# Low-rank and gate matrices of a diffusion block padded with zero rows to 128

## The chip, the cores and the metric

The kernel runs on one core of one Trainium2 chip. Its time is device microseconds of one execution. Three runs of the kernel before gave 2284.68, 2291.41 and 2297.06 us; the median, 2291.41 us, is its time. In the profile, PE is TensorE's matmul, PEld its weight load, DVE VectorE, ACT ScalarE, POOL GpSimd and SP the engine that issues most transfers.

## The reference

One layer of a hybrid diffusion backbone over 256 latent tokens and 256 context tokens, 2048 channels wide: a modulated norm, one input projection, two token mixers side by side (a bidirectional RWKV-7 scan with 16 heads of 64, and a bidirectional chunked gated DeltaNet with 8 heads of 128), a gated merge, an output projection and a SwiGLU feed-forward block. The change touches the RWKV features and readout:

```
lora_w = einsum('btdr,drc->btdc', tanh(wd.reshape(b, t, 2, 96)), w2)      # 2 directions, rank 96
decay  = exp(-exp(-softplus(-(w0 + lora_w)) - 0.5))
iclr   = sigmoid(a0 + einsum('btdr,drc->btdc', ad.reshape(b, t, 2, 96), a2))
gate   = sigmoid(gd) @ g2                                                 # rank 64
...
return (yn + bonus) * gate
```

`wd` and `ad` are 2 x 96 columns each of the input projection, `gd` is 64 columns, and each of `w2`, `a2` and `g2` maps a rank to 1024 channels.

## The kernel before, in words

Activations lie with channels on the 128 partitions and tokens along the free dimension: 512 tokens (latent, then context), or the 256 latent ones.

The first stage (to about 132 us) makes the modulation vectors and the modulated activations, and accumulates in six PSUM tiles, `low`, the first projections: four groups of 96 low-rank columns among them, with 64 gate columns and 32 DeltaNet columns in the rows that are left over. The last two stages (from about 1312 us) merge the branches, project and run the feed-forward block. They consist of projections in three products each: weights and activations are split into a high and a low part in fp32r, high x high, high x low and low x high.

The stage between is where the change lies. Its order on PE, DVE, ACT and POOL is not that of the code: generators yield operations, and a planner, `Weave`, picks at each step the operation that could start first by its own books, with a rank to break ties. Its books hold a cost for each operation (`Lane.__getattr__`), a time at which each engine is free, and events that generators wait for. A matmul's cost is a fixed share plus so much per column, with a factor 1.22 for 96 rows (L137); an operation on POOL costs 0.06 + 0.0024 us per element of a partition. Each engine then runs its instructions in the planned order and waits on semaphores where the data is not there. SP is left to the framework's own scheduler.

The generators of that stage:

- `lowrank` (L718) makes the activations of the four low-rank groups. `shift` mixes each token with its neighbours, with one operation on ACT and six on DVE, and writes 96 rows of `lin`, a view of a tile with the tag KB. Then it works in four bursts of eight products of 96 rows: for each pair `p` of RWKV heads four products `w[:96]` by `lin`, out to one of two PSUM banks with the tag s (`psb`). Each is emptied by `lowrank_out` (L710): a sigmoid on ACT into `lo`, then a write to DRAM issued from ACT. One load of `lora` serves a burst. Before the second burst it makes `sgd`, the 64 rows of the gate's activations.
- `prepare`, `grams`, `inverse`, `values` and `scan` run the eight pairs. The first `prepare` waits for its pair's low-rank rows, the second one for all of them. At the end of `scan` (L983 to L987) stands the gate product: a load of 64 rows of `g2`, one product with `sgd`, 256 columns wide, and a copy by ACT.
- `features`, `tokens`, `decays`, `head_grams`, `head_inverse` and `head_scan` run the eight DeltaNet heads, after the pairs. `ada_rest` runs beside them on DVE.
- `products` (rank 900, last of all) does the remaining input projections. `cast` splits each weight piece into `whi` on ACT and `wlo` on DVE. A projection is 48 matmuls, 512 or 256 columns wide. They are the work that fills PE while the others wait.

All helpers' operations carry line 145, where a planned operation is issued; `dq` loads carry L156. Arrays are laid out on the host: `lora` as 4 x 96 x 8 x 128, `g2` as 64 x 1024.

Of the kernel before, what the change touches and what calls it, by code (L numbers as in the profile page):

```python
# [11 lines left out]
F32 = mybir.dt.float32  # L12
F32R = mybir.dt.float32r
AF = mybir.ActivationFunctionType
# [4 lines left out]
P = 128  # L19
D = 2048  # L20
KT = D // P
T = 256
# [88 lines left out]
class Lane:  # L111
# [5 lines left out]
    def __getattr__(self, name):  # L117

        def op(out, *a, **k):
            if name == "preload_act_table_set":  # L120
                return Op(self, 1.3, lambda: self.engine.preload_act_table_set(out))
            if name == "dma_start":
                return Op(self, 0.6 if self.each > 0.002 else 0.06, lambda: self.engine.dma_start(out, *a))
            n = int(np.prod(out.shape[1:]))
            kind = "full"
            if name == "transpose" and len(a) == 2:
                cost = 0.109
            elif name == "matmul":
                rows, m = a[0].shape[0], out.shape[0]
                if a[0].dtype == F32R:  # L130
                    cost, kind = 0.0035 + 0.000448 * n, "split"
                elif rows <= 64 and m <= 64:
                    cost, kind = 0.026 if rows < 64 else max(0.06, 0.05 + 0.00015 * n), (rows, m)
                elif m <= 64:
                    cost, kind = 0.085 if m == 64 else 0.12, (rows, m)
                else:
                    cost = (0.0054 + 0.00167 * n) * (1.22 if rows == 96 else 1)  # L137
            else:
                psum = a and getattr(a[0], "tensor", None) is not None and "PSum" in type(a[0].tensor).__name__
                cost = (self.psum if psum else self.fixed) + self.each * n  # L140
                if name == "tensor_tensor_scan":
                    cost *= 1.9
                elif name == "scalar_tensor_tensor" and not psum:
                    cost *= 1.2
            return Op(self, cost, lambda: getattr(self.engine, name)(out, *a, **k), kind)  # L145
        return op
# [124 lines left out]
def emit(ctx: ExitStack, tc, A, out, dbg=None):  # L271
    nc = tc.nc
    V, S, G, Q = nc.vector, nc.scalar, nc.gpsimd, nc.sync
# [3 lines left out]
    dq = Loads(Q)  # L277
    e, v, s = Lane(E, 0.0, 0.0, 0.0), Lane(V, 0.07, 0.00104, LAT["own"], 0.13), Lane(S, 0.09, 0.00086, LAT["own"], 0.165)
    g = Lane(G, 0.06, 0.0024, LAT["own"])
# [129 lines left out]
    with tc.tile_pool(name="p0", bufs=1) as p0, \  # L409
# [31 lines left out]
        ps = pst(pa, "pa")  # L441
# [263 lines left out]
    for b in (pib, mmb, psb, psb, mmb, pab):  # L705
        b.free.pop()
    pr[0]["kps"], pr[0]["rps"] = low[4], low[5]
    sgd = rs.tile([64, T], F32, tag="sgd", name="sgd")

    def lowrank_out(p, j, ps, so):  # L710
        yield s.activation(so, ps, AF.Sigmoid, bias=p_("w0" if j < 2 else "a0", 8 * (j % 2) + p))
# [6 lines left out]
    def lowrank():  # L718

        yield s.preload_act_table_set(SIGM)  # L720
        lin = rs.tile([P, 2, 8, 2, 64], F32, tag="KB", name="lin", bufs=2).rearrange("p a b c d -> p (a b c d)")[:96].rearrange("p (j t) -> p j t", j=4)
        raw = rs.tile([P, 4, 64], F32, tag="Y", name="raw").rearrange("p a b -> p (a b)")[:64]
        ab = rs.tile([P, 512], F32, tag="XT", name="ab")[:32]
        for j, b in ((0, pib), (2, psb), (1, mmb), (3, psb)):
            ps = low[j]
            yield from shift(ps, 96, 24 + j, lin[:, j])
            if j < 2:
                yield s.activation(lin[:, j], lin[:, j], AF.Tanh)
                yield s.copy(raw[32 * j:32 * j + 32], ps[96:P, 0:T])
            if j == 2:  # L730
                yield s.copy(ab, ps[96:P])
                Q.dma_start(abd.rearrange("b r t -> r b t"), ab.rearrange("r (b t) -> r b t", b=4))
            weave.release(b)
        out = [rs.tile([P, 8, 2, 64], F32, tag=f"VX{i}", name="lo").rearrange("p a b c -> p (a b c)") for i in range(2)]
        out = [t[:, n:n + 512] for t in out for n in (0, 512)]
        for p in range(NPAIR):
            if p == 2:
                yield from shift(raw, 64, 28, sgd, ctx_part=False)
                yield s.activation(sgd, sgd, AF.Sigmoid)
                yield "prepared", 0, 1  # L740
                yield s.preload_act_table_set(SIGM)
            if p % 2 == 0:
                w = wp.tile([P, 8, P], F32, tag="wraw", name="wraw", bufs=3)
                yield dq(w[:96], A["lora"][p // 2])
            for j in (0, 2, 1, 3):
                ps = yield psb
                yield e.matmul(ps, w[:96, 4 * (p % 2) + j], lin[:, j], start=True, stop=True)
                weave.add(2, lowrank_out(p, j, ps, out[j]))

    def prepare(p):  # L750
# [152 lines left out]
    def scan(p):  # L903
# [76 lines left out]
        weave.ready("scan", p)  # L980

        Yf = Y.rearrange("p c t -> p (c t)")
        g2 = rs.tile([P, P], F32, tag="gate", name="g2")[:64]  # L983
        Q.dma_start(g2, A["g2"][:, P * p:P * p + P])
        ps = yield pab
        yield e.matmul(ps[:, T:], g2, sgd, start=True, stop=True)
# [659 lines left out]
def layouts(x, c, ctx, c_ctx, w_ada, b_ada, norm1_w, w_in, rw_mu, rw_w0, rw_w2, rw_a0, rw_a2,  # L1646
# [67 lines left out]
                                             (3360, 96), (1024, P), (0, P))]  # L1714
    A["w_low"] = np.ascontiguousarray(np.concatenate(lows, 2).reshape(P, 8, 2, 736).transpose(1, 0, 2, 3))
    lw = np.concatenate([np.asarray(rw_w2[0], f), np.asarray(rw_a2[0], f)], 0)
    A["lora"] = np.ascontiguousarray(lw.reshape(4, 96, 4, 2, P).transpose(2, 1, 3, 0, 4)).reshape(4, 96, 8, P)
    A["g2"] = np.asarray(rw_g2[0], f)
    A["pa"] = cols(merge_p_a[0], [P * j for j in range(KT)])
    A["pb"] = cols(merge_p_b[0], [P * j for j in range(KT)])  # L1720
    A["wout"] = cols(w_out[0], [P * j for j in range(KT)])
# [18 lines left out]
```

## Time and profile before

| what | value |
| --- | --- |
| median of three runs | 2291.41 us (2284.68 to 2297.06) |
| profiled execution, its span | 2286.3 us (the page gives no other time of it) |
| mean granted clock of TensorE | 0.985 |
| POOL, busy | 110.3 us |
| DMA queues, share of 16 engines' span | 49.5% SP and ACT, 7.1% POOL, 3.3% a third |

The profile is one execution. A f32 product stands in it as two records with a load each, an fp32r product as one. Matmuls are pipelined, so that a record lasts longer than the distance to the next one: distances between starts tell what a product costs. A row of a group gives the line, engine, operation, out<-in and the shape, where 96*128 means 96 active rows and 128 active columns; then the busy time, the mean in ns, and the idle time of the engine ahead of it with what ended it. A row of the order of time gives start and length in us, and in brackets the idle time ahead of it and its releaser. A row of busy time by stretches gives the stretch, its length, the busy time of PE, PEld, DVE, ACT and POOL with their numbers of instructions, the granted clock, the DMA share and GB/s.

### The profile page before, as it was taken

How to read it: one execution, taken by the hardware profiler on the slowest of the kernel's cores; microseconds unless marked ns; L12 is line 12 of the kernel's file. 1: busy time of each engine (PE TensorE's matmuls, PEld its weight loads, DVE VectorE, ACT ScalarE, POOL GpSimd, SP SyncE). 2: the span in 40 equal slices, each digit the busy share in tenths (PEclk: the TensorE clock that was granted, in tenths of full speed). 3: DMA queues.
4: the chain of work that ended last, by engine and by line, in shares of the span. 5: the costliest groups of instructions: out<-in, count | busy, mean ns of one | idle time of the engine just before them, and what ended most of it. 6: DMA issues, size and time to landing. Idle time of an engine off the chain costs nothing. (4 is left out here: it accounts for less than half of the span.)

```text
span 2286.3 us, 54678 instructions
## 1 busy us (share of the span) xinstructions
PE 2184.5 (96%) x22904; PEld 1925.0 (84%) x22904; DVE 1561.3 (68%) x3225; ACT 1056.6 (46%) x1922; POOL 110.3 (5%) x185
## 2 busy tenths in 40 slices
PE   7998999999999999999999989899999999999998
PEld 4766577777777788888888889889999999999997
DVE  3446588888877586899997668774656656444444
ACT  3245554544555554444453445444444444444443
POOL 0000000000000010111110040000000000000000
PEclk9999999999999999999999989999999999999999
DMA  9955643443443254555566696864777776566665
GB/s 384 407 148 170 187 113 89 117 106 99 106 101 100 87 180 141 162 163 165 167 188 216 232 350 230 283 207 142 237 238 236 236 233 214 186 185 192 186 189 162
DMA packets 231926, 430.76 MB, mean 188 GB/s; under 512 B 114944, under 2 KB 129152, under 8 KB 227328
## 3 DMA queue, kind: packets, MB, share of 16 engines
q1 hardware_dynamic: 203744, 350.72, 49.5%
q0 software_dynamic: 14112, 51.39, 7.1%
q10 hardware_dynamic: 13824, 25.17, 3.3%
q8 instruction: 179, 2.93, 0.5%
q14 instruction: 67, 0.55, 0.1%
HBM read 401.44 MB, written 25.77 MB: 187 GB/s over the span
## 5 line engine op out<-in xcount | busy, mean ns | idle before, releaser
L361 DVE TENSOR_TENSOR wlo<-wraw,whi 128x1024 fp32r<-128x1024 f32 x328 | 393.4, 1199 | 336.5 <-ACT whi L360 332.9
L360 ACT CAST whi<-wraw 128x1024 fp32r<-128x1024 f32 x328 | 337.5, 1029 | 469.2 <-PE mm L371 434.4
L145 PE MATMUL mm<-hxh,wlo 128*128 128x256 f32 (+1 forms) x1376 | 466.3, 339 | 7.3 <-DVE wlo L145 6.9
L145 PE MATMUL mm<-hxh,whi 128*128 128x256 f32 (+1 forms) x1376 | 464.7, 338 | 6.0 <-ACT whi L145 5.8
L145 PE MATMUL mm<-hxl,whi 128*128 128x256 f32 (+1 forms) x1376 | 462.2, 336 | 0.0
L372 PE MATMUL mm<-hfh,wlo 128*128 128x256 f32 x1344 | 374.9, 279 | 0.3 <-DVE wlo L361 0.3
L370 PE MATMUL mm<-hfh,whi 128*128 128x256 f32 x1344 | 374.9, 279 | 0.0
L371 PE MATMUL mm<-hfl,whi 128*128 128x256 f32 x1344 | 374.7, 279 | 0.0
L145 PEld LDWEIGHTS mm<-hxh,wlo 128*128 128x128 f32 x1376 | 262.4, 191 | 35.5 <-DVE wlo L145 10.0
L145 PEld LDWEIGHTS mm<-hxh,whi 128*128 128x128 f32 x1376 | 262.6, 191 | 33.3 <-ACT whi L145 7.2
L145 PEld LDWEIGHTS mm<-hxl,whi 128*128 128x128 f32 x1376 | 262.3, 191 | 25.2 <-issue 5.7
L145 DVE TENSOR_TENSOR wlo<-wraw,whi 128x512 fp32r<-128x512 f32 x344 | 236.1, 689 | 59.3 <-ACT whi L145 58.0
L372 PEld LDWEIGHTS mm<-hfh,wlo 128*128 128x128 f32 x1344 | 252.7, 188 | 0.5 <-DVE wlo L361 0.5
L370 PEld LDWEIGHTS mm<-hfh,whi 128*128 128x128 f32 x1344 | 252.8, 188 | 0.0
L371 PEld LDWEIGHTS mm<-hfl,whi 128*128 128x128 f32 x1344 | 252.7, 188 | 0.0
L145 ACT CAST whi<-wraw 128x512 fp32r<-128x512 f32 x344 | 205.0, 618 | 94.2 <-PE mm L145 56.9
L145 DVE TENSOR_TENSOR arena<-arena 128x512 f32<-128x512 f32 (+12 forms) x538 | 132.9, 248 | 28.2 <-DMA arena<-scr 13.5
L370 PE MATMUL mm<-za,whi 128*128 128x256 f32 x512 | 142.9, 279 | 0.0
L372 PE MATMUL mm<-za,wlo 128*128 128x256 f32 x512 | 142.7, 279 | 0.0
L371 PE MATMUL mm<-za,whi 128*128 128x256 f32 x512 | 142.7, 279 | 0.0
L370 PEld LDWEIGHTS mm<-za,whi 128*128 128x128 f32 x512 | 96.3, 188 | 0.0
L371 PEld LDWEIGHTS mm<-za,whi 128*128 128x128 f32 x512 | 96.3, 188 | 0.0
(318 smaller groups left out, 3907.5 us busy)
## 6 DMA issues: line engine op xcount, KB each, us to landing
wraw<-w SPq DMA_DIRECT2D x172, 512.0 KB, 4.1
wraw<-wgu SPq DMA_DIRECT2D x168, 512.0 KB, 4.5
aw<-ada_rest POOLq DMA_DIRECT2D x96, 512.0 KB, 5.2
aw<-ada_first SPq DMA_DIRECT2D x32, 1024.0 KB, 11.6
wraw<-wdn SPq DMA_DIRECT2D x64, 448.0 KB, 3.6
wraw<-wout SPq DMA_DIRECT2D x32, 512.0 KB, 4.8
aw<-ada_gt ACTq DMA_DIRECT2D x64, 256.0 KB, 4.8
wraw<-wdn SPq DMA_DIRECT2D x32, 512.0 KB, 3.6
```

The source lines that it names most:

```text
L145: return Op(self, cost, lambda: getattr(self.engine, name)(out, *a, **k), kind)
L360: S.copy(hi[:, c, :M], raw[:, c, :M])
L361: V.tensor_sub(lo[:, c, :M], raw[:, c, :M], hi[:, c, :M].bitcast(F32))
L370: E.matmul(ps, hi, Xh[:, k, :n], start=first and i == 0, stop=False)
L371: E.matmul(ps, hi, Xl[:, k, :n], start=False, stop=False)
L372: E.matmul(ps, lo, Xh[:, k, :n], start=False, stop=last and i == len(wt) - 1)
```

## The change

`lora` gets 32 rows of zeros on the host and `g2` gets 64. `lin` keeps its whole tile of 128 rows, and POOL clears the rows 96 to 127 (as a planned operation, ahead of the first `shift`); `sgd` becomes a tile of 128 rows, whose rows 64 to 127 POOL clears before the planned stage. The products and loads then take 128 rows; `shift`, tanh and sigmoid still write 96 and 64. The planner's factor for 96 rows is taken out.

```
-                    cost = (0.0054 + 0.00167 * n) * (1.22 if rows == 96 else 1)
+                    cost = (0.0054 + 0.00167 * n)
...
-    sgd = rs.tile([64, T], F32, tag="sgd", name="sgd")
+    sgd = rs.tile([P, T], F32, tag="sgd", name="sgd")
+    G.memset(sgd[64:P], 0.0)
...
-        lin = rs.tile([P, 2, 8, 2, 64], F32, tag="KB", name="lin", bufs=2).rearrange("p a b c d -> p (a b c d)")[:96].rearrange("p (j t) -> p j t", j=4)
+        lin = rs.tile([P, 2, 8, 2, 64], F32, tag="KB", name="lin", bufs=2).rearrange("p a b c d -> p (a b c d)").rearrange("p (j t) -> p j t", j=4)
+        yield g.memset(lin[96:P], 0.0)
...
-            yield from shift(ps, 96, 24 + j, lin[:, j])
+            yield from shift(ps, 96, 24 + j, lin[:96, j])
             if j < 2:
-                yield s.activation(lin[:, j], lin[:, j], AF.Tanh)
+                yield s.activation(lin[:96, j], lin[:96, j], AF.Tanh)
...
-                yield s.activation(sgd, sgd, AF.Sigmoid)
+                yield s.activation(sgd[:64], sgd[:64], AF.Sigmoid)
...
-                yield dq(w[:96], A["lora"][p // 2])
+                yield dq(w, A["lora"][p // 2])
             for j in (0, 2, 1, 3):
                 ps = yield psb
-                yield e.matmul(ps, w[:96, 4 * (p % 2) + j], lin[:, j], start=True, stop=True)
+                yield e.matmul(ps, w[:, 4 * (p % 2) + j], lin[:, j], start=True, stop=True)
...
-        g2 = rs.tile([P, P], F32, tag="gate", name="g2")[:64]
+        g2 = rs.tile([P, P], F32, tag="gate", name="g2")
...
-    A["lora"] = np.ascontiguousarray(lw.reshape(4, 96, 4, 2, P).transpose(2, 1, 3, 0, 4)).reshape(4, 96, 8, P)
-    A["g2"] = np.asarray(rw_g2[0], f)
+    A["lora"] = np.pad(lw.reshape(4, 96, 4, 2, P).transpose(2, 1, 3, 0, 4).reshape(4, 96, 8, P), ((0, 0), (0, 32), (0, 0), (0, 0)))
+    A["g2"] = np.pad(np.asarray(rw_g2[0], f), ((0, 64), (0, 0)))
```

## The prediction

> **What bounds the kernel now.** I read the page first, then busy time by stretches, then the order of time around the operations that the change touches.
>
> ```profile
> span 2286.3 us, 54678 instructions
> PE 2184.5 (96%) x22904; PEld 1925.0 (84%) x22904; DVE 1561.3 (68%) x3225; ACT 1056.6 (46%) x1922; POOL 110.3 (5%) x185
> ```
>
> ```profile
> core 0: us, PE busy (x) PEld busy (x) DVE busy (x) ACT busy (x) POOL busy (x), PEclk, DMA share, GB/s
> ...
> 134.00:253.00 119.00, 103.75 (x615) 72.78 (x616) 69.16 (x157) 67.81 (x115) 2.90 (x6) 0.94 0.61 181
> 253.00:888.00 635.00, 616.74 (x8723) 480.68 (x8724) 497.63 (x1235) 319.83 (x770) 27.08 (x59) 0.99 0.43 116
> 888.00:1231.00 343.00, 333.89 (x3525) 286.35 (x3524) 310.33 (x799) 170.03 (x339) 38.61 (x59) 1.00 0.59 175
> 1231.00:1312.00 81.00, 73.99 (x796) 70.30 (x794) 53.31 (x136) 31.42 (x69) 5.23 (x10) 0.94 0.61 194
> ```
>
> The stage that the change touches is the planned mixing stage, from 134 us to 1312 us. PE is busy for 1128.4 of its 1178 us; 49.6 us are waits of PE: 15.2 in the first stretch (where all low-rank products lie), 18.3 while the RWKV pairs run, 9.1 in the middle of the DeltaNet heads, 7.0 in the last stretch. PE runs its instructions in the planned order, and in the built programs, before and after, the stage's last PE instruction is an input projection, so free work lasts to the end. The stage's time is therefore PE's work, plus the cost of switching between shapes, plus waits. A microsecond off PE counts only if no wait takes its place; off the other engines it counts only through waits. DVE is the runner-up: 310.33 of 343.00 us (90.5%) in the head stretch.
>
> **Part 1, the 32 low-rank products (96 rows to 128).** Here is the first burst of eight, PE's records first, weight loads and ACT then.
>
> ```profile
> 160.96 0.42 PEld L145 LDWEIGHTS s<-lin,wraw 96*128 96x128 f32 x2
> 161.63 0.19 PEld L145 LDWEIGHTS s<-lin,wraw 96*128 96x128 f32 x1 [0.24 <-issue]
> 162.06 0.19 PEld L145 LDWEIGHTS s<-lin,wraw 96*128 96x128 f32 x1 [0.24 <-issue]
> ...
> 162.99 0.30 PEld L145 LDWEIGHTS s<-lin,wraw 96*128 96x128 f32 x2 [0.75 <-ACT lo L145]
> ```
>
> ```profile
> 162.25 0.69 ACT L145 ACTIVATE lo<-s,PR 128x512 f32<-128x512 f32 x1 [3.55 <-PE s L145]
> 162.97 0.35 ACTq L123 DMA_DIRECT2D sgd__1342<-lo  x1
> 163.37 0.69 ACT L145 ACTIVATE lo<-s,PR 128x512 f32<-128x512 f32 x1 [0.43 <-PE s L145]
> 164.09 0.33 ACTq L123 DMA_DIRECT2D sgd__1342<-lo  x1
> ```
>
> ```profile
> 261.48 0.42 PEld L145 LDWEIGHTS pa<-arena,C 128*128 128x128 f32 x2
> 262.14 0.19 PEld L145 LDWEIGHTS mm<-hxl,whi 128*128 128x128 f32 x1 [0.24 <-issue]
> 262.57 0.19 PEld L145 LDWEIGHTS mm<-hxh,wlo 128*128 128x128 f32 x1 [0.24 <-issue]
> ```
>
> An f32 product is two records. While nothing holds them up, 96-row records follow each other in 0.43 us (161.63 to 162.06). The same product with 128 rows also takes 0.43 a record (262.14 to 262.57), and a load is 0.19 in both. So 96 rows are not slower than 128. What makes the rest of the burst slow is the third product, which waits for `lo`: a product needs a bank of tag s, there are two, and ACT empties one in 0.69 and then issues the write in 0.33 to 0.35, so that evictions start 1.12 apart (162.25 to 163.37). PE would need 0.86. Padding leaves eviction and write as they are: the term is 0. Bounds: if ACT did not set the pace, 1.12 - 0.86 = 0.26 saved on each of 32, 8.3 us; on the other side 0, since both shapes run at 0.43 a record when nothing holds them up, and a loss would have to show there.
>
> **Part 2, the eight gate products (64 rows to 128).** The first fence is one of them between projections, the second a 128-row product of the same width.
>
> ```profile
> 405.77 0.28 PE L145 MATMUL mm<-hxh,whi 128*128 128x256 f32 x1
> 405.89 0.28 PE L145 MATMUL mm<-hxl,whi 128*128 128x256 f32 x1
> 406.10 0.70 PE L145 MATMUL pa<-sgd,g 64*128 64x256 f32 x2
> 406.72 0.38 PE L145 MATMUL mm<-hxh,wlo 128*128 128x256 f32 x1
> 406.95 0.28 PE L145 MATMUL mm<-hxh,whi 128*128 128x256 f32 x1
> ```
>
> ```profile
> 474.02 0.28 PE L145 MATMUL mm<-hxh,whi 128*128 128x256 f32 x1
> 474.14 0.59 PE L145 MATMUL pa<-Y,C 128*128 128x256 f32 x2
> 474.38 0.47 PE L145 MATMUL mm<-hxl,whi 128*128 128x256 f32 x1
> 474.68 0.28 PE L145 MATMUL mm<-hxh,wlo 128*128 128x256 f32 x1
> ```
>
> From the last projection before to the second after it is 406.95 - 405.89 = 1.06 us with 64 rows and 474.68 - 474.02 = 0.66 with 128. The difference of 0.40 is the price of going into another array shape and out again. Eight of them: -3.2 us (bounds -3.2, and 0 where PE would wait there anyway). The Trainium skill, "TensorE: Matmul & The Clock Gate", section "Why this matters for your kernels", says that a product of few rows takes the time of a full one; by that rule the eight would give 0. The Trainium skill, "TensorEngine Tiling (Array Packing)", section "Key Properties", says that a change of tiling mode drains the engine; by that rule they give something, and the two fences side with it (0.40 each). For 96 rows the first rule holds.
>
> **Part 3, what the planner makes of it.** The stage's order is written by a planner from costs in the code. The change gives it two new numbers: 96-row products without the factor 1.22, and POOL's clearing of `lin`, 0.06 + 0.0024 x 2048 = 5.0 us in its books, ahead of the low-rank work. In the built programs the order differs almost everywhere after that. I counted, over the stage:
> - Changes of array shape from one PE instruction to the next: 666 before, 667 after. The 16 around the gate products are gone, 17 others came. At half of 0.40 each: +3.4 (lower bound: a change costs only the 0.21 - 0.12 = 0.09 seen on entering, 405.89 to 406.10 against 405.77 to 405.89: +1.5).
> - Projections ahead of the first low-rank burst: 204 instead of 141; ahead of the fourth: 437 instead of 406. The chain of pairs starts later behind work that had to be done anyway. Also casts now stand between evictions in two bursts. The front's 15.2 us of waits could shrink or grow: term 0, bounds -5 to +4 (a third and a quarter of them).
> - Projections between the head chain's first and 37th state update, the stretch from 888 to 1231 us: 1041 instead of 1322. The 281 missing are 256 wide, 0.12 us each: 33 us of PE work move to where the heads don't run. DVE's casts there fall from 110 to 86.
>
> ```profile
> L145 DVE TENSOR_TENSOR wlo<-wraw,whi 128x512 fp32r<-128x512 f32 x344 | 236.1, 689 | 59.3 <-ACT whi L145 58.0
> ```
>
> So DVE loses 24 x 0.689 = 16.5 us there and PE 33: DVE 293.8, PE 300.9. If PE still waited 9.1 us, the stretch would be 310.0 and DVE 94.8% busy instead of 90.5%. Can it? One half of a head shows it can come near:
>
> ```profile
> 974.00:1004.00 30.00, 29.29 (x410) 24.45 (x409) 29.79 (x62) 12.06 (x29) 4.36 (x8) 1.00 0.69 206
> ```
>
> DVE 99% busy, and PE waited 0.7 us. Bounds for the added wait: 0, if every part went so; and if DVE stayed at 90.5%, the stretch is 293.8 / 0.905 = 324.6, which is +14.6. I take +3, near the lower end, because the row above is nearer to the case.
>
> **Part 4, clears and loads.** POOL does two clears that wait for the tiles of the stage before, like its next instruction does now:
>
> ```profile
> 132.42 0.11 POOL L786 MEMSET arena<- 128x8 f32 x1 [131.48 <-PE pa L372]
> 193.26 1.39 POOL L818 COPY bon<-arena 128x256 f32<-128x256 f32 x1 [60.72 <-DVE arena L145]
> ```
>
> ```profile
> L145 POOL MEMSET TF<- 128x1024 f32 x2 | 1.9, 952 | 3.5 <-ACT whi L145 3.5
> ```
>
> 1024 elements per partition take 0.95, so 2048 and 256 take about 2.2 us, from 132.4 to 134.6. Behind them on POOL stand the small clear at L786 and then nothing until 193; the product that waits for `lin` comes after 161. Hidden, with some 26 us to spare; if that cover went, 2.2. The clears write other partitions than ACT's evictions into `lin`, and in the built program those carry no wait for POOL. The four low-rank loads grow from 384 to 512 KB, the eight gate loads from 32 to 64 KB:
>
> ```profile
> wraw<-w SPq DMA_DIRECT2D x172, 512.0 KB, 4.1
> ...
> wraw<-lora SPq DMA_DIRECT2D x4, 384.0 KB, 3.7
> ```
>
> At the size of the first row they land 0.4 later. PE waits on such a load once in the stage (0.5 us); I add 0.4 (bounds 0 and 1.6, all four exposed).
>
> **Sum.** 0 - 3.2 + 3.4 + 0 + 3 + 0.4 = +3.6 us on a span of 2286.3. The page gives this execution no other time than its span; it lies 5.1 us under the median of the three runs, 2291.41 (2284.68 to 2297.06), so I add the sum to the median: 2295.0 us.
>
> **The rivals.**
> - *The head stretch is DVE's.* If DVE cannot get past 90.5% where the heads run, 33 us of projections leave and 14.6 us of waits come. Sum: -3.2 + 3.4 + 14.6 + 0.4 = +15.2, time 2306.6, slower by 0.7%. It decides once those waits grow by more than 11 us. For it: 90.5% over 343 us is the highest share of any stretch. Against it: the half head at 99%, and that the 24 casts leave too.
> - *The front fills up.* The first burst now stands behind 7.7 us more of projections (60 of 0.12, three of twice that), which can cover PE's waits in the first 119 us. If two thirds of the 15.2 go: -10.1 - 3.2 + 1.5 + 0.4 = -11.4, time 2280.0, faster by 0.5%. Against it: much of those waits is inside the bursts, where ACT sets the pace.
> - *Rows were what slowed the bursts*, as the planner's factor says: -8.3 - 3.2 + 3.4 + 0.4 = -7.7, time 2283.7. The 0.43 us of both shapes speaks against it.
> - *The padding does nothing at all*, as the first rule above has it: 3.2 more than my sum, 2298.2, within my forecast.
>
> **How the numbers follow.** About 0.5%, 11.5 us, is what a measurement of this kernel can tell from no change. Forecast (waits in the head stretch up by 0 to 8, front within its bounds): 0.52. DVE rival: 0.24. Front: 0.16. Rows: 0.08. Faster by over 0.5% is most of the front case: 0.17. Slower by over 0.5% is most of the DVE case and a little of the forecast's upper end: 0.25. Within: 0.58. The range goes from the front case with a little more, 2277, to the DVE case with the upper bound of the front (+4), 2311.
>
> **What would show it.** Right, if in the profile after: 128-row low-rank records still run in pairs 1.1 us apart with `lo` on ACT as releaser; the gate product with its neighbours takes 0.66 instead of 1.06; POOL's clears end near 135 us and nobody waits for them; the head stretch is shorter by 20 to 33 us with DVE above 92%. Wrong, if the low-rank bursts drop to 0.9 us a product (rows mattered), if the gate product still takes 1.06, if the head stretch keeps its length (DVE bound it), or if PE's waits in the first 119 us move by more than 5 us.

## The result and the profile after

The changed kernel takes 2312.7 us (median of four runs, 2310.34 to 2316.6); the kernel before, now with a fourth run, 2289.6 (2284.68 to 2297.06). The ratio is 1.0100, with a 95% interval of 1.0079 to 1.0122: **slower by 1.0%, 23 us**, where +3.6 us was predicted with a range up to 2311. The profiled execution has a span of 2308.5 us, 22.2 more than before. One execution in this study, of the kernel with a delay of 1.5 us further down, took 4152.5 us with no cause known; it is left out of that kernel's time and ratio.

The page of the changed kernel, span and busy time of each engine:

```profile
span 2308.5 us, 54697 instructions
PE 2198.9 (95%) x22904; PEld 1934.1 (84%) x22904; DVE 1566.6 (68%) x3225; ACT 1058.9 (46%) x1922; POOL 113.6 (5%) x187
```

Set beside the same two lines of before, this already splits the loss. PE has the same 22904 instructions and is busy 14.4 us longer (2198.9 - 2184.5). Its idle time, span less busy, grew by 7.8 us (109.6 against 101.8). Together that is the 22.2. The mean granted clock is 0.979 instead of 0.985, and 2308.5 x 0.021 - 2286.3 x 0.015 = 14.2 us, as much as PE's busy time grew. So by this account nearly two thirds of the growth is time at a lower clock, a quantity that the prediction's sum doesn't have at all. It is an account of two executions; what a full clock would win back is another question, and the runs answer it with less (below).

Busy time by stretches, in the changed kernel; the columns are the stretch, its length, busy time of PE, PEld, DVE, ACT and POOL, granted clock, DMA share, GB/s. The cuts are the same events as before: last low-rank product, first and 37th state update of the heads, first product of the merge, first of the feed-forward block.

```profile
134.00:263.00 129.00, 111.08 (x646) 79.55 (x647) 76.44 (x168) 71.35 (x122) 2.31 (x6) 0.94 0.60 184
263.00:925.00 662.00, 641.65 (x8913) 506.05 (x8912) 510.73 (x1249) 329.53 (x787) 29.58 (x59) 0.98 0.42 117
925.00:1249.00 324.00, 309.64 (x3239) 256.44 (x3238) 290.08 (x769) 157.26 (x311) 40.67 (x58) 0.98 0.53 162
1249.00:1330.00 81.00, 77.15 (x861) 73.80 (x860) 57.81 (x142) 34.42 (x75) 6.05 (x11) 1.00 0.68 221
1330.00:1554.00 224.00, 199.13 (x1559) 192.62 (x1558) 165.66 (x207) 108.20 (x156) 32.38 (x45) 0.94 0.78 273
```

The head stretch is the third row: 324 us instead of 343, clock 0.98 instead of 1.00, and DVE at 290.08 / 324 = 89.5%, where 92% or more was expected. The second row, the pairs, is 662 instead of 635 us and has 0.98 instead of 0.99. Counting the records between those events gives this account, after less before, in us. A projection is counted at the distance between starts, 0.12 (256 wide) or 0.235 (512 wide); clock is half of the time at half clock; the rest is what is left.

| stretch | length | projections | PE's waits | clock | rest |
| --- | --- | --- | --- | --- | --- |
| 134 us to the first state update | +36.3 | +25.8 | +4.8 | +8.5 | -2.8 |
| first to 37th state update | -18.5 | -33.7 | +5.3 | +6.8 | +3.1 |
| to the first merge product | -0.2 | +7.9 | -3.2 | -5.1 | +0.2 |
| merge, to the feed-forward block | +4.5 | 0 | +2.3 | +3.5 | -1.3 |
| sum | +22.1 | 0 | +9.2 | +13.7 | -0.8 |

The projections' column adds up to nothing: they were only moved. They came to the pairs (and 7.9 us of them to the end) and left the heads. In the pairs the time grew by all of them and more; at the end it did not grow. Where they left, 33.7 us of work went and 18.5 us were won. (Outside these stretches PE waited 1.3 us less than before, which makes the 7.8 of the page.) The merge stage, whose code the change doesn't touch, took between 220.3 and 230.2 us in the traces of this study, so its +4.5 can't be told from its own spread.

How the clock goes down is seen in three neighbouring stretches of 3.4 us in the head stretch, and in PE's order of time there (start, length, idle time ahead in brackets):

```profile
946.50:949.90 3.40, 3.17 (x73) 1.73 (x71) 3.40 (x9) 1.90 (x4) 0.81 (x1) 1.00 0.00 0
949.90:953.30 3.40, 2.07 (x70) 1.52 (x71) 3.36 (x10) 0.79 (x2) 0.28 (x1) 1.00 0.03 7
953.30:956.70 3.40, 3.40 (x17) 2.36 (x19) 3.34 (x8) 1.96 (x6) 0.00 (x0) 0.50 0.06 10
```

```profile
950.76 0.73 PE L145 MATMUL pi<-arena,Tx 32*32 32x16 f32 x64 [1.00 <-DVE arena L145]
951.42 0.50 PE L145 MATMUL mm<-hxh,whi 128*128 128x512 f32 x1
951.75 0.40 PE L145 MATMUL mm<-hxl,whi 128*128 128x512 f32 x1
952.62 0.50 PE L145 MATMUL mm<-hxh,wlo 128*128 128x512 f32 x1 [0.46 <-DVE wlo L145]
...
954.35 0.63 PE L145 MATMUL mm<-hxh,wlo 128*128 128x512 f32 x1
954.78 0.63 PE L145 MATMUL mm<-hxh,whi 128*128 128x512 f32 x1
955.20 0.63 PE L145 MATMUL mm<-hxl,whi 128*128 128x512 f32 x1
```

Two waits, 1.00 and 0.46 us, leave PE busy for 2.07 of 3.40 us. In the next 3.40 us PE is never idle, yet the granted clock is 0.50, and the 512-wide projections start 0.43 apart (954.35, 954.78, 955.20). At full clock they start 0.235 apart (the fence on the gate product, below). Three more such windows stand in this stretch, at 1005, 1056 and 1110 us, and one just ahead of it at 899, each behind a wait in or just before a head's inverse. Before, the head stretch had none.

Parts 1, 2 and 4 as the changed kernel's rows show them: weight loads of the first low-rank burst, ACT in it, and POOL's clears.

```profile
170.41 0.19 PEld L145 LDWEIGHTS s<-lin,wraw 128*128 128x128 f32 x1 [0.24 <-issue]
170.84 0.19 PEld L145 LDWEIGHTS s<-lin,wraw 128*128 128x128 f32 x1 [0.24 <-issue]
171.78 0.30 PEld L145 LDWEIGHTS s<-lin,wraw 128*128 128x128 f32 x2 [0.75 <-ACT lo L145]
```

```profile
171.04 0.69 ACT L145 ACTIVATE lo<-s,PR 128x512 f32<-128x512 f32 x1
171.76 0.35 ACTq L123 DMA_DIRECT2D sgd__1342<-lo  x1
172.16 0.69 ACT L145 ACTIVATE lo<-s,PR 128x512 f32<-128x512 f32 x1 [0.43 <-PE s L145]
```

```profile
116.67 0.31 POOL L709 MEMSET sgd<- 64x256 f32 x1 [115.72 <-PE mm L458]
117.03 1.81 POOL L145 MEMSET lin<- 32x2048 f32 x1
133.17 0.12 POOL L788 MEMSET arena<- 128x8 f32 x1 [14.33 <-PE pa L372]
```

With 128 rows a low-rank record still takes 0.43 us (170.41 to 170.84), the third product still waits for `lo`, and evictions are still 1.12 apart (171.04 to 172.16). The clears are done at 118.8 us; nothing on PE or ACT waits for them.

PE's order of time ahead of a gate product of the changed kernel, which also gives the 0.235 used above:

```profile
495.03 0.39 PE L145 MATMUL mm<-hxh,whi 128*128 128x512 f32 x1
495.26 0.40 PE L145 MATMUL mm<-hxl,whi 128*128 128x512 f32 x1
495.50 0.40 PE L145 MATMUL mm<-hxh,wlo 128*128 128x512 f32 x1
495.82 0.73 PE L145 MATMUL pi<-arena 32*32 32x16 f32 x64
496.48 0.70 PE L145 MATMUL pa<-sgd,g 128*128 128x256 f32 x2
```

The gate product here stands between 32x32 products: in the new order its neighbours are others than before, so its own gain has to be measured in a kernel that keeps the order (below).

### The profile page after: what moved, and what is told of

Same layout as the page of the kernel before. It is cut to its first block, busy times and chain, and to the rows that moved or that the text cites. A ratio compares the mean times of both kernels' runs of the same rounds, so it can differ in the third digit from the quotient of the medians.

```text
span 2308.5 us, 54697 instructions
## 1 busy us (share of the span) xinstructions
PE 2198.9 (95%) x22904; PEld 1934.1 (84%) x22904; DVE 1566.6 (68%) x3225; ACT 1058.9 (46%) x1922; POOL 113.6 (5%) x187
## 4 chain that ended last, share of the span: by engine, by line
PE 56%; DVE 7%; DMA 5%; issue 3%; ACT 2%; SPq 1%; POOL 0%; DVEq 0%; ACTq 0%; POOLq 0%
PE mm L372 13%; PE mm L370 12%; PE mm L371 12%; PE mm L145 12%; PE s L145 3%; PE pa L145 2%; DVE arena L145 2%; DMA wr<-wgu 1%; DVE wlo L145 1%; PE pi L145 1%; DMA scr<-T 1%; DVE aw L145 1%; DMA arena<-scr 1%; DMA wraw<-pa 1%; DVE wlo L361 1%
## 5 line engine op out<-in xcount | busy, mean ns | idle before, releaser
L145 DVE TENSOR_TENSOR arena<-arena 128x512 f32<-128x512 f32 (+13 forms) x538 | 133.4, 249 | 21.8 <-DMA arena<-scr 9.1
```

## The experiments

The theory after the result: **the order** that the planner wrote costs the time, not the padding. The first rival: the padded products, clears and loads cost it. The second: DVE sets the pace in the head stretch, as the prediction's rival had it.

### Order against padding

All of the padding in the order of before: the factor stays in the books, the clear of `lin` is issued outside the planner, the load is priced as before.

```
+        G.memset(lin[96:P], 0.0)
...
+                yield dq(w, A["lora"][p // 2], 0.75)
...
+                op = e.matmul(ps, w[:, 4 * (p % 2) + j], lin[:, j], start=True, stop=True)
+                op.cost *= 1.22
+                yield op
```

> Both matrices padded and both clears made, but the planner is told the old costs (1.22 kept for the 32 low-rank products, the clear of lin made outside the planner), so that PE, DVE, ACT and POOL keep the order of the kernel before through the whole mixing stage. Theory A (the new order costs the 23 us, the padding nothing): time of before less 3.2 us for the eight gate products, about 2286 us, ratio 0.9986, and no half-clock stretches between 888 and 1231 us. Theory B (the padding itself costs, by larger loads, longer reads of 128 rows, or POOL's clears): close to the changed kernel, about 2310 us, ratio 1.009.

The same, cut to the gate matrix and `sgd` alone:

```
-    sgd = rs.tile([64, T], F32, tag="sgd", name="sgd")
+    sgd = rs.tile([P, T], F32, tag="sgd", name="sgd")
+    G.memset(sgd[64:P], 0.0)
...
-        g2 = rs.tile([P, P], F32, tag="gate", name="g2")[:64]
+        g2 = rs.tile([P, P], F32, tag="gate", name="g2")
```

> Only the gate's matrix and its activations padded to 128 rows; order of before kept in the mixing stage. Both theories: the gate product with its neighbours takes 0.66 us instead of 1.06, eight of them 3.2 us; time 2286 us, ratio 0.9986. If a rule that rows cost nothing holds for 64 rows too: ratio 1.000 and 1.06 us stay.

And cut to the low-rank matrices alone (the first diff without the gate's lines):

> Only the low-rank matrices and activations padded to 128 rows; the order of PE, DVE and ACT is exactly that of before. My step (the bursts are paced by the evictions): ratio 1.000, eviction starts 1.1 us apart in the first burst as before. If rows slow the products (the planner's factor 1.22): 8.3 us less, ratio 0.9964, and products 0.86 us apart. If larger loads cost: up to 1.6 us more.

The new order without any padding: products keep 96 and 64 rows, but the books hold what the changed kernel's hold, with a planned clear of the 32 unused rows of the tile.

```
-                    cost = (0.0054 + 0.00167 * n) * (1.22 if rows == 96 else 1)
+                    cost = (0.0054 + 0.00167 * n)
...
+        yield g.memset(lin[96:P], 0.0)
+        lin = lin[:96].rearrange("p (j t) -> p j t", j=4)
...
+                yield dq(w[:96], A["lora"][p // 2], 4 / 3)
```

> Matrices and products as before (96 and 64 rows), but the planner is told the changed kernel's costs (no factor 1.22, the planned clear of lin ahead of the low-rank work), so that the mixing stage has the changed kernel's order. Theory A: slower than before like the changed kernel, plus 3.2 us for the gate products that stay at 64 rows: about 2315 us, ratio 1.011; half-clock stretches once per head again. Theory B: about 2290 us, ratio 1.000.

| kernel | us | ratio to before (95%) |
| --- | --- | --- |
| all padding, old order | 2295.64 | 1.0014 (1.0003 to 1.0026) |
| gate alone | 2291.26 | 1.0006 (0.9990 to 1.0021) |
| low-rank alone | 2299.82 | 1.0032 (1.0019 to 1.0045) |
| new order, no padding | 2314.21 | 1.0099 (1.0081 to 1.0118) |

The pages of the padded kernel in the old order, and of the unpadded one in the new order:

```profile
span 2293.7 us, 54682 instructions
PE 2183.5 (95%) x22904; PEld 1925.1 (84%) x22904; DVE 1563.6 (68%) x3225; ACT 1056.9 (46%) x1922; POOL 110.6 (5%) x187
```

```profile
span 2311.3 us, 54694 instructions
PE 2202.6 (95%) x22904; PEld 1933.7 (84%) x22904; DVE 1565.9 (68%) x3225; ACT 1059.5 (46%) x1922; POOL 113.2 (5%) x186
```

These two pages look as if PE's busy time went with the order: 2183.5 padded in the old order (2184.5 before), 2202.6 unpadded in the new one (2198.9 in the changed kernel). They can't carry that, since busy time also goes with the clock of the one execution that was profiled: 0.988 for the first of them. The page of the gate alone, in the old order, comes from an execution at 0.980:

```profile
span 2299.6 us, 54681 instructions
PE 2198.4 (96%) x22904; PEld 1939.4 (84%) x22904; DVE 1564.8 (68%) x3225; ACT 1057.7 (46%) x1922; POOL 108.1 (5%) x186
```

It is the ratios that settle the first rival: all of the padding is worth 0.1%, the order 1.0%. In the head stretch the padded kernel in the old order is the kernel before again:

```profile
888.00:1231.00 343.00, 334.50 (x3530) 287.06 (x3529) 310.63 (x800) 169.93 (x339) 38.95 (x59) 1.00 0.59 175
```

This stretch repeats well from trace to trace. In five executions with the order of before or nearly so (before, the three padded kernels of this section, and the delay of 1.5 us below) it lasts 342 to 344 us, with 8.5 to 9.1 us of PE's waits and at most 3.4 us at half clock. In four with the new order (the changed kernel twice, the new order without padding, and the delay of 1.87 us below) it lasts 324 to 328 us, with 14 to 17 us of waits and 10 to 17 us at half clock, whether the matrices are padded or not.

The gate product alone, PE's order of time:

```profile
406.08 0.28 PE L145 MATMUL mm<-hxh,whi 128*128 128x256 f32 x1
406.19 0.28 PE L145 MATMUL mm<-hxl,whi 128*128 128x256 f32 x1
406.32 0.59 PE L145 MATMUL pa<-sgd,g 128*128 128x256 f32 x2
406.56 0.47 PE L145 MATMUL mm<-hxh,wlo 128*128 128x256 f32 x1
406.87 0.28 PE L145 MATMUL mm<-hxh,whi 128*128 128x256 f32 x1
```

From the last projection before it to the second after it: 406.87 - 406.19 = 0.68 us, where 64 rows took 1.06. Counted so, five of the eight win 0.38 to 0.39 against the kernel before and the other three 0.19 to 0.28: 2.6 us of PE in all. The changed kernel wins 2.4 on its eight against the new order without padding, where the neighbours are the same. The time doesn't show it: 2.6 us are 0.11%, and the interval reaches from -0.10 to +0.21%.

The low-rank padding by itself is slower by 0.3%, with the order of before, where 0 was expected and 1.6 us at most. Its loads and its clear were not tried apart, and its trace doesn't point at them: of the 13.9 us that its span has over before, 3.9 lie between 134 us and the first state update, where all its products are, and 10.2 in the merge and the feed-forward block, which the padding doesn't touch. All of the padding in the old order also missed its 0.9986, by 0.3%.

### How little tips the order

The changed kernel with only the clear of `lin` taken out of the planner, so that the missing factor alone acts on the books:

```
-        yield g.memset(lin[96:P], 0.0)
+        G.memset(lin[96:P], 0.0)
```

> Both matrices padded, factor 1.22 out, but the clear of lin made outside the planner: a third order, with 1099 projections' matmuls in the head stretch. Theory A1: between, nearer to the changed kernel: 223 x 0.117 = 26 us of work leave the heads, waits and half clock give back some 10: 2298 to 2306 us, ratio 1.003 to 1.007. Rival A2: anywhere above 1.000, without relation to the heads. If only the clear's place in the plan matters: 1.000 to 1.002, like the padded kernel in the old order.

The kernel before with nothing but a delay in the planner's books ahead of the low-rank work, 1.5 us in one kernel and 1.87 in the other; no instruction is added:

```
+        yield 1.5
```

> The kernel before with nothing padded and nothing cleared; the planner is only told that the low-rank work starts 1.5 us later than it would. In the built program PE's order differs from that of before in 17 lines, all ahead of the second low-rank burst, and the heads hold 1322 projections' matmuls as before. Theory C (the clear's place in the books tips one choice, and the order behind that choice is what costs): ratio 1.000, within 0.2%. Theory D (a later start of the low-rank chain costs by itself, in proportion): 1.5/5.0 of the changed kernel's 1%: ratio 1.003.

```
+        yield 1.87
```

> The same with 1.87 us, what the clear of lin takes on the chip. Nothing is padded or cleared. In the built program the choice has tipped: the key projection of the second pair stands ahead of the second burst instead of behind it, and from the pairs on the order is the changed kernel's (1041 matmuls in the heads, 307 lines of PE differ from it in all). Theory C: ratio 1.008 to 1.012, half-clock stretches in the heads. Theory D: 1.87/5.0 of 1%, ratio 1.004, and no step from the kernel with 1.5.

The factor alone gives a third order (1099 projections in the head stretch): 2304.51 us, 1.0054 (1.0034 to 1.0074). The delay of 1.5 us keeps the order of before but for 17 lines of PE: 2298.53, 1.0036 (1.0023 to 1.0049). The delay of 1.87 us gives the changed kernel's order from the pairs on: 2311.68, 1.0091 (1.0078 to 1.0104). The page of the last one:

```profile
span 2310.4 us, 54685 instructions
PE 2201.9 (95%) x22904; PEld 1933.7 (84%) x22904; DVE 1562.8 (68%) x3225; ACT 1058.9 (46%) x1922; POOL 111.2 (5%) x185
```

Nothing is padded and nothing cleared in it, and yet it loses most of what the change lost: 0.37 us in the books are worth 13 us on the chip. That step is theory C's; theory D, with 1.003 and 1.004, has none. But C expected no loss at 1.5 us, and the 0.36% there stays unexplained. In the built programs the key projection of the second pair moves: it stands ahead of the second low-rank burst instead of behind it, and all later choices follow. Heads 0 to 4 lose about one gate projection each: each has 46 to 61 products 256 wide where it had 80 to 129, beside some 96 that are 512 wide.

### Where the free work lies

If the loss comes from the heads having too little free work, giving it back should repair it. The changed kernel with the gate projections' places rewritten, so that the head stretch holds 1307 projections again (1322 before, 1041 after):

```
-GATES_A, GATES_B = ((6, 3, 0, 2, 3, 3, 1, 3), (3, 0, 0, 0, 0, 2, 6, 8))
+GATES_A, GATES_B = ((6, 3, 0, 2, 3, 1, 0, 2), (3, 1, 1, 1, 1, 2, 6, 8))
```

> The changed kernel, with four of the free gate projections released later in the planner's lists (one for each of the heads 1 to 4 instead of pairs 5 to 7): in the built order the stretch from the first to the 37th state update holds 1307 projections' matmuls instead of 1041 (before: 1322). Theory A1 (the heads lack free work: with none left PE waits in each head long enough that the clock is halved once a head): the half-clock stretches of the heads go, the head stretch is about 341 us with about 9 us of waits, and the time comes back to 2288 to 2296 us, ratio 1.000. Rival A2 (any other order than the one before loses, wherever the free work lies; the loss sits in the pairs too): still 2303 or more, ratio 1.006 or more.

The kernel before with the heads starved to 1018:

```
-GATES_A, GATES_B = ((6, 3, 0, 2, 3, 3, 1, 3), (3, 0, 0, 0, 0, 2, 6, 8))
+GATES_A, GATES_B = ((8, 4, 0, 2, 3, 3, 1, 3), (0, 0, 0, 0, 0, 2, 6, 8))
```

> The kernel before (nothing padded, planner's costs untouched), with three gate projections released at the first pairs instead of at head 0: the same stretch holds 1018 projections' matmuls instead of 1322. Theory A1: the heads lose their free work, half-clock stretches appear about once a head, the head stretch shrinks by some 20 us and not by the 35.6 us of PE work that leave it (304 x 0.117), time 2302 to 2312 us, ratio 1.005 to 1.010. If lack of free work in the heads is harmless: ratio 1.000.

The changed kernel with the key projection of the second pair put back behind the second burst:

```
-                todo.append(("k", p, ("rdone", p - 1)))
+                todo.append(("k", p, ("rdone", p - 1) if p > 1 else ("lowrank", 1)))
```

> The changed kernel with that one choice turned back by hand: the key projection of the second pair may only be taken once the second low-rank burst is through. In the built order it stands between bursts 2 and 3, as before, and the second pair's readout comes behind the same projections; but from the seventh pair on the order falls back into the changed kernel's, with 1041 matmuls in the heads. If the loss is made in the pairs' first part: ratio 1.004 or less. If it is made by the heads having no free work: ratio 1.007 or more, stretch of the heads about 324 us with half-clock stretches.

| kernel | us | ratio to before (95%) | head stretch | its waits, time at half clock |
| --- | --- | --- | --- | --- |
| heads refilled | 2319.08 | 1.0114 (1.0090 to 1.0138) | 336.5 | 8.8, 0 |
| heads starved | 2320.62 | 1.0122 (1.0104 to 1.0140) | 329.4 | 24.6, 17.1 |
| later key projection | 2313.92 | 1.0100 (1.0079 to 1.0122) | 327.3 | 15.3, 17.1 |

The pairs and the heads of the refilled kernel:

```profile
263.00:917.00 654.00, 625.52 (x8713) 486.56 (x8712) 498.55 (x1238) 323.48 (x771) 28.65 (x59) 0.98 0.41 112
917.00:1253.00 336.00, 327.16 (x3503) 282.46 (x3502) 303.53 (x785) 164.89 (x333) 38.51 (x59) 1.00 0.59 177
```

The heads are repaired: clock 1.00, and 8.8 us of waits, as before. But the pairs now have 654.0 - 625.5 = 28.5 us of waits where the changed kernel has 20.3, and from 134 us to the first state update there are 51 us at half clock, against 38 in the changed kernel and 20 before. The whole is no faster. So "the heads have too little" is only half of it: in this order the free work pays in neither of the two places where it was put. Starving the heads of the kernel before does to them what the change did, and more: 24.6 us of waits instead of 14.4, and a time above the 2302 to 2312 us that theory A1 gave. The key projection alone does not bring the old order back.

### Does DVE set the pace where the heads run?

In both kernels the 120 multiply-adds of the modulation on DVE work on 128 of 512 elements, with their price in the books kept, so that the order stays.

```
-                    yield v.scalar_tensor_tensor(a, w[:, n:n + 512], ck[:, k, 0:1], a, ALU.mult, ALU.add)
+                    op = v.scalar_tensor_tensor(a, w[:, n:n + 512], ck[:, k, 0:1], a, ALU.mult, ALU.add)
+                    op.call = lambda a=a[:, :128], i=w[:, n:n + 128]: V.scalar_tensor_tensor(a, i, ck[:, k, 0:1], a, ALU.mult, ALU.add)
+                    yield op
```

> The changed kernel in its own order, but the 120 multiply-adds of the modulation rows, which DVE does beside the heads (90 of them inside the head stretch, 0.67 us each), work on 128 of their 512 elements; the rest is left out, and the planner is told the old cost. DVE loses about 38 us inside the head stretch. Theory A3 (in the new order DVE is what PE waits for in the heads, and those waits bring the half clock): the head stretch falls from 324.5 us to 310 or less, its half-clock stretches go, and the time falls by 10 to 16 us, to about 2299 us, ratio 1.000 to 1.005. Rival A4 (the head's own chain of steps paces it, whatever DVE has to do beside): head stretch above 320 us, time 2306 or more, ratio 1.0075 or more.

> The kernel before with the same work left out of the same multiply-adds, in its own order. Its head stretch has free projections enough that PE waits 9.1 of 343 us. Theory A3: little to win, 2 to 5 us, ratio 0.998 to 0.999. If it gains as much as the changed kernel does, lighter DVE helps any order and the comparison says nothing of the new one.

The changed kernel with lighter DVE takes 2312.71 us, 1.0100 (1.0076 to 1.0124): nothing gained. The kernel before takes 2282.28, 0.9954 (0.9937 to 0.9972): 9 us gained, where 2 to 5 were expected. The head stretch, first of the changed kernel with lighter DVE, then of the kernel before with it:

```profile
928.00:1247.00 319.00, 304.63 (x3240) 253.45 (x3239) 258.91 (x767) 156.32 (x310) 38.27 (x59) 0.99 0.54 165
```

```profile
889.00:1224.00 335.00, 331.43 (x3522) 285.90 (x3521) 275.40 (x798) 169.97 (x339) 38.64 (x59) 1.00 0.59 180
```

In the changed kernel DVE drops to 258.91 / 319 = 81%, and PE's waits stay at 14.4 us, as in the changed kernel itself: **DVE's load does not make them.** So the second theory falls. The stretch is 5 us shorter all the same, just between what the theory and its rival gave; by the account that is the clock (3.4 us at half clock instead of 13.7), and the whole time doesn't show it. What PE waits for there, in the changed kernel (waits of PE from 925 to 1249 us: total, times, longest):

```profile
PE pa L145 <- ACT arena L145: 3.5, 5, 1.0
PE pi L145 <- DVE T L145: 3.2, 3, 1.3
PE s L145 <- DVE Vn L145: 1.8, 4, 1.2
PE pi L145 <- DMA T<-tscr: 1.3, 2, 1.0
```

And in the kernel before (from 888 to 1231 us):

```profile
PE pa L145 <- ACT arena L145: 3.5, 4, 1.0
PE pi L145 <- DVE arena L145: 1.6, 3, 1.3
```

These are steps of one head's chain, each waiting for the step ahead of it. The largest of them is the same in both kernels. What is new is waits inside the inverse, for `T` (3.2 us) and for its transfer (1.3). That points to too few projections between two steps in the planned order, though each head still has some 145; it is argued, not tried. In the kernel before DVE was in part the bound: with it lighter, PE's waits there fell from 9.1 to 3.6 us.

### Does half clock cost time there?

The account puts more on the clock than on waits, but a window at half clock may fall into time that the chain leaves free anyway. So the waits that bring it were filled with work that nobody reads: two products of 128 x 256 into a free half of the inverse's bank, ahead of six products, once where PE waits (heads 0 to 4) and once where it doesn't (heads 5 to 7). The order stays. The changed kernel ran again beside them.

```
+        def filled(ops, g):
+            for at in warm.get(g, ()):
+                ops[at].call = lambda c=ops[at].call: [E.matmul(ps[:, 256:512], ident, c_("rmask"), start=True, stop=True) for _ in range(2)] and c()
+            return ops
...
-                                           8, h % 2, True, v)
+                                           8, h % 2, True, v, {0: {1: (16,)}, 1: {2: (0,)}, 2: {1: (16,)}, 3: {1: (16,)}, 4: {1: (2, 16)}}.get(h, {}))
```

The second of the two filled kernels differs in the last line alone:

```
+                                           8, h % 2, True, v, {5: {1: (16,), 2: (0,)}, 6: {1: (16,), 2: (0,)}, 7: {1: (16,), 2: (0,)}}.get(h, {}))
```

> The changed kernel again, on the chip of the next two kernels and with more runs than before, as the base for them. Every theory: 2310 to 2316 us, the granted clock 0.978 to 0.981, and four or five windows of 3.41 us at half clock between 895 and 1115 us, each behind a wait of PE in a head's inverse.

> The changed kernel, its order kept, with two products of 128 x 256 that nobody reads ahead of six products of the heads' inverses, at the places where PE waited 0.85 to 1.44 us in the trace of the changed kernel (heads 0 to 4). They add about 0.86 us each place, 5.2 us, and lie inside the waits. Theory C (a window of 3.41 us in which PE is idle for over 1.3 us is followed by one at half clock, and PE sets the pace in it): the five halved windows of the heads go, 5 x 1.71 = 8.5 us, the fillers take back 0 to 2: 6 to 8 us less than the changed kernel in the same call, and the stretch from the first to the 37th state update 317 to 319 us instead of 324.5. Rival W (the heads' chain sets the pace in those windows, so that half clock costs nothing there): the windows may go, the time stays within 2 us of the changed kernel.

> The same six pairs of products put where PE does not wait: heads 5, 6 and 7, the same two places of the inverse. This prices a filler. Theory C: PE has no time to spare there, so 6 x 0.86 = 5.2 us and up to 6 x 0.40 for the changes of shape: 5 to 8 us more than the changed kernel, with the halved windows of heads 0 to 4 still there. Rival W: the chain has room, 0 to 2 us more.

| kernel | us | ratio to before (95%) | head stretch | its waits, time at half clock |
| --- | --- | --- | --- | --- |
| the changed kernel again | 2317.93 | 1.0098 (1.0071 to 1.0125) | 328.4 | 16.0, 17.1 |
| filled where PE waits | 2309.71 | 1.0085 (1.0051 to 1.0118) | 324.9 | 12.1, 6.8 |
| filled elsewhere | 2322.19 | 1.0118 (1.0091 to 1.0146) | 329.7 | 12.6, 23.9 |

The head stretch of the second and of the third:

```profile
925.00:1250.00 325.00, 312.89 (x3266) 259.01 (x3264) 290.38 (x768) 156.16 (x309) 40.92 (x58) 0.99 0.54 162
```

```profile
927.00:1257.00 330.00, 317.31 (x3261) 263.26 (x3260) 291.34 (x768) 156.11 (x309) 40.38 (x59) 0.96 0.53 159
```

All windows at half clock behind the filled waits are gone; the one of 6.8 us that is left lies at 1142 us, behind a wait that was not filled. The two kernels have the same work and nearly the same waits there; the one with 17.1 us less at half clock is 4.8 us shorter in this stretch, where 8.5 would be the whole of it. That speaks for theory C with part of its price, but it doesn't show it: it is one trace of each, and the changed kernel's own two traces, 324.5 and 328.4, lie 3.9 apart. That the windows went because the waits were filled isn't shown either, since the new order without padding, with nothing filled, had none of the first two in its trace. The stretch of 317 to 319 us that theory C expected was missed; the filled kernel still waits 12.1 us there. In the median it is 8.2 us under the changed one (6 to 8 expected), and the other filled kernel 4.3 over it (5 to 8), but the intervals overlap.

The runs on record say more, as each has its own granted clock. Take the 169 executions of this study that come with a clock, the long one left out, and set each against the mean of its kernel on its chip: one whose clock is 0.01 lower took 13 us longer (standard error 1.6; for the 70 of the kernel before alone it is 16, with 2.4). If each microsecond at half clock cost the half that PE loses, it would be 0.01 x 2300 = 23. So half clock goes with lost time, at a little over half of its full price. This is a relation between executions and not a trial of its own. As an estimate by it, the 0.006 by which the clock of the two profiled executions differs is worth some 8 us of the 22, and not 14. Why half clock goes with less than its full price stays open.

## Why the prediction was wrong, point by point

- **Part 1, low-rank products, 0: the pace right, the price not borne out.** 0.43 us a record with 128 rows, evictions 1.12 apart, `lo` as releaser. But the low-rank padding alone, in the old order, is slower by 0.3% (0.19 to 0.45%), some 7 us, and its trace doesn't show where.
- **Part 2, gate products, -3.2: right in the main on PE,** 2.6 us where the order is kept and 2.4 in the new one. It is too small for the runs to show.
- **Part 3, changes of shape, +3.4: not shown.** The rest of the account moved by +0.5 us up to the merge; parts 2 and 3 together had +0.2 there.
- **Part 3, front, waits 0 (-5 to +4): within its bounds.** 15.2 us to 129.0 - 111.1 = 17.9 from 134 us to the last low-rank product.
- **Part 3, the price of the projections that leave the head stretch, taken at +3 us of waits: this is the step that failed.** 33.7 us of projections left, as counted, and 18.5 were won: 15.2 lost, of which 5.3 waits, 6.8 clock and 3.1 rest. So the waits were mis-sized by little (+3 against 5.3, and 5 to 8 in the four executions with this order), and by the account the larger part of the loss is the clock, which the sum has no term for, and a rest. Of the 18.6 us between the sum (+3.6) and the growth of the span (+22.2), 12.2 lie in this stretch, 9.9 ahead of it (where the sum's other terms belong), -8.1 behind it and 4.5 in the merge. The upper bound, 324.6 us, is met to 0.1, but that is luck: its reason, a DVE that can't be fuller, doesn't hold. The row with DVE at 99% showed that DVE can be full while PE hardly waits. It did not show what happens when a head has fewer projections between two steps of its chain. DVE's share went down, not up, and lighter DVE left the waits alone.
- **Moved work was taken as neutral elsewhere; it wasn't.** From 134 us to the first state update 25.8 us more of projections made 36.3 us. The pairs took 21 of them (328.4 - 307.3 between the first gate product and the first state update) and got 3 us more waits and 5 more of clock with them. The end of the stage gave 8 us back: 7.9 us more projections, the same length.
- **The granted clock was left out of the sum.** By the account it is 14 of the 22 us of the span, and by the relation between executions some 8. Its rows were on the table: the rows by stretches of before showed 0.94 in the two where PE waited for 13 and 9% of the time, and 0.99 and 1.00 in the two where it waited for 3%.
- **Part 4: the price right, the place wrong.** 0.31 + 1.81 = 2.1 us (2.2 expected), but from 116.7 instead of 132.4: the clears did not wait for what POOL's next instruction waits for. The loads of `lora` land 0.3 later (4.0 against 3.7), 0.4 expected. But PE waited for them for 2.3 us instead of 0.5, 1.8 more and so over the bound of 1.6; in the new order with the smaller loads it waited 1.9, so that their size isn't shown to be the cause.
- **The rivals.** The DVE rival came nearest with 2306.6, by a mechanism that the lighter DVE refutes. Rows did not slow the bursts, the front's waits did not shrink, and the padding does something, on PE.
- **Why all this came from padding:** the planner's books. A clear on POOL that takes 1.81 us and that nobody waits for stands at 5.0 in them, and the order tips between 1.5 and 1.87. The missing factor alone gives an order that loses half as much.

Still open: why this order does worse with its free work in both places where it was put, rather than by how much; how much of the loss a full clock would win back; the 0.1 to 0.4% by which kernels with the order of before, or nearly so, differ from it; and the merge stage's own spread. No kernel that does all the work beat the kernel before; the gate matrix alone, in the old order, ties with it.

## What to carry to other kernels

Where a planner writes the order, a change of data is also a change of its books: keep the order fixed (price the new operation as the old, issue a hidden one outside the planner) before judging the change itself, and judge the new order by a run of its own. Work that fills PE is not neutral when it moves: price a stretch that loses it by its chain's steps, not by the share of the busiest other engine. And put the granted clock in the sum: a stretch where waits gather can lose time a second time by it.

## What the runs showed of the hardware

- **Half clock behind scattered waits.** From 134 to 1554 us of the changed kernel, windows of half clock last 3.41 or 6.83 us and all start on one grid of 3.41 us; the grid lies elsewhere in each execution. Cut on that grid, 392 windows at full clock remain: 18 were followed by half clock, and PE was idle in them for 1.33 us or more, by the records, whose ends are modelled; 374 were not, and the most idle of these had 1.62. In other executions a few windows with 0.7 to 1.2 us of idle time were followed too, so it is not a sharp rule. The Trainium skill, "TensorE: Matmul & The Clock Gate", section "What's actually happening", gives a free-running window of 3413 ns, and the traces agree (3.41). The Trainium skill, on the same page, section "HAM oscillation — how this bites in real kernels", states as the rule that idle gaps of PE should not exceed about 3.4 us; here a window with gaps of 1.00 and 0.46 us was followed by half clock, and the measurement decides.
- **Price of half clock.** An execution whose granted clock is 0.01 lower than its kernel's mean took 13 us longer (169 executions), where 23 would be the full price.
- **The same waits fall into other windows each time.** Because the grid lies elsewhere, the same kernel had 13.7 us at half clock in its head stretch in one execution and 17.1 us in another, and the window at 899 us came in the first alone. Part of what one kernel's runs differ by, 2310.34 to 2316.6 here, may come from this; it was not separated.
- **Clears on POOL:** 0.31 us for 64 rows of 256 elements, 0.95 for 128 rows of 1024 (in the kernel before), 1.81 for 32 rows of 2048; their price goes with the elements of a row, not with the rows.
